# A diffusion-layer kernel on one core: the first modulation weights are loaded amid the tokens, their row is made between the sums of squares, and log, exp and the first products go segment by segment

## The chip, the cores and the metric

The kernel runs on one core of a Trainium2 chip. The metric is the device time of one execution in microseconds (us). Engines are named as in the profile: PE (matrix products), PEld (its weight loads), DVE (vector), ACT (scalar), POOL (GpSimd) and SP (which only issues DMAs here). Each engine works through its own instructions in the order in which they stand and waits for others by semaphores.

## What is computed

One layer over 1024 latent tokens and 256 context tokens of width 1024. The beginning, which the change touches, is this part of the reference:

```
mod_x = (jax.nn.silu(c) @ w_ada[i] + b_ada[i])[:, None, :]
mod_c = jax.nn.silu(c_ctx) @ w_ada[i] + b_ada[i]
sh1, sc1, g1, sh2, sc2, g2 = jnp.split(mod_x, 6, axis=-1)
csh1, csc1, cg1, csh2, csc2, cg2 = jnp.split(mod_c, 6, axis=-1)

px = modulate(rms_norm(x, norm1_w[i]), sh1, sc1) @ w_in[i]
pc = modulate(rms_norm(ctx, norm1_w[i]), csh1, csc1) @ w_in[i]
```

`rms_norm(x, w)` is `x * rsqrt(mean(x*x) + EPS) * w`, and `modulate(h, shift, scale)` is `h * (1 + scale) + shift`. Behind it come a gated DeltaNet on half of the heads, neighbourhood attention on the other half, an output projection and a SwiGLU network, none of which the change touches.

## The kernel before, in words

The tokens stand transposed: 8 tiles `xt0` to `xt7`, each with 128 of the 1024 channels as partitions and all 1280 tokens as columns (256 context tokens, then 1024 latent ones). The columns are worked on in three segments (`SEGS`) of 256, 512 and 512, since a bank of PSUM holds 512.

SP loads, in this order: the 8 token tiles (640 KB each, L680), the first two weight blocks `fraw0` and `fraw1` (512 KB each, L684), three tiles `wada` of modulation weights (1024 KB each, L676), two tables of constants, the other five `wada`, and small tables.

In the stage around the change, the order on PE, DVE and ACT is that of the code (a manual schedule); behind it a scheduler orders them.

- Sums of squares (L737 to L742). Token tiles go in pairs. ACT squares both, DVE adds the two squares, PE multiplies the sum with a matrix of ones, three matmuls (one per segment) that accumulate over the four pairs in three banks. In the last pair the second square and the addition go segment by segment.
- `rs` (L744, L745). ACT takes the logarithm of each segment's mean, and one exponential over all 1280 columns gives the reciprocal root.
- Weight split (L201, L204). A weight block is split into `whi` (rounded to the fast type) and `wlo` (the rest), on DVE for the first block, on POOL for the second.
- The row of tile j: `ada(j)` (L706) multiplies the two SiLU vectors with `wada` j on PE, and a copy (L708) takes the row `arow` out of PSUM. `column(j)` turns the row into columns with small PE matmuls (L714); DVE adds the bias (L716) and makes the scale `w1s` (L719).
- `normed_tile(k)`. DVE multiplies a token tile by `w1s` and `rs` (L726), ACT adds the shift and rounds to `hh` (L727), DVE makes the rest `hl` (L729). For tile 0 it goes over the three segments, for the others over 256 and 1024 columns.
- First products (L757). Two blocks of outputs, `first[0]` and `first[1]`, need for every tile k the products `whi`·`hh`, `wlo`·`hh` and `whi`·`hl`. For tile 0 they are written out in the stage itself, six matmuls for each of the three kinds, one block after the other. `ada(1)` stands ahead of them, `column(1)` and `normed_tile(1)` behind the first kind, `ada(2)` and `column(2)` behind the last.
- Then tiles 1 to 7 (L413), with `ada` 3 to 7 and their columns between the blocks (table `AHEAD`).

Of the kernel before, what the change touches and what calls it, by code (L numbers as in the profile page):

```python
# [9 lines left out]
F32 = mybir.dt.float32  # L10
# [3 lines left out]
AF = mybir.ActivationFunctionType  # L14
OP = mybir.AluOpType
# [73 lines left out]
def hybrid(ctx, tc, a, dbg):  # L89
# [293 lines left out]
    with ExitStack() as bs:  # L383
# [282 lines left out]
        with ExitStack() as xs:  # L666
            xp = pools(xs, "xp", "left")
            xt = []
# [5 lines left out]
            def load_ada(j):  # L674
                aw[j] = w = wap.tile([128, KT, 256], F32, name="wada", tag="wada")
                sp.dma_start(w, a["wa1"][j])  # L676

            for k in range(KT):
                x = xp.tile([128, T], F32, name=f"xt{k}", tag=f"xt{k}")
                sp.dma_start(x, a["xcT"][k])  # L680
                xt.append(x)
            raws = [xp.tile([128, KT, 128], F32, name=f"fraw{i}", tag=f"fraw{i}") for i in range(2)]
            for i in range(2):
                sp.dma_start(raws[i], a["w_conv"][4 + i])  # L684
            for j in range(3):
                load_ada(j)
# [33 lines left out]

            def normed_tile(k, cuts=(slice(0, CT), slice(CT, T))):
                t = xt[k]
                parts = [(x, mod1[:, k, int(x.start < CT):int(x.start < CT) + 1]) for x in cuts]
                for x, sh in parts:
                    j = int(x.start < CT)
                    dve.scalar_tensor_tensor(t[:, x], t[:, x], w1s[:, k, j:j + 1], rs[:, x], op0=OP.mult, op1=OP.mult)  # L726
                    act.activation(hh[k][:, x], t[:, x], AF.Identity, bias=sh)  # L727
                for x, sh in parts:
                    dve.scalar_tensor_tensor(hl[k][:, x], t[:, x], sh, hh[k][:, x].bitcast(F32),  # L729
                                             op0=OP.add, op1=OP.subtract)  # L730

            with tc.manual_schedule(engines={mybir.EngineType.PE, mybir.EngineType.DVE, mybir.EngineType.Activation}):
                sums = [bank() for _ in SEGS]
                segs = [slice(s0, s0 + n) for s0, n in SEGS]
                for k in range(0, KT, 2):
                    sq = [xp.tile([128, T], F32, name="sq%d" % i, tag="sq%d" % i, bufs=2 + i) for i in range(2)]
                    act.activation(sq[0], xt[k], AF.Square)  # L737
                    for s in segs if k == KT - 2 else [slice(0, T)]:
                        act.activation(sq[1][:, s], xt[k + 1][:, s], AF.Square)
                        dve.tensor_tensor(sq[1][:, s], sq[0][:, s], sq[1][:, s], OP.add)  # L740
                    for p, s in zip(sums, segs):
                        pe.matmul(p[:, :s.stop - s.start], M[C_ONE], sq[1][:, s], start=k == 0, stop=k == KT - 2)  # L742
                for p, s in zip(sums, segs):
                    act.activation(rs[:, s], p[:, :s.stop - s.start], AF.Ln, bias=b_eps, scale=1.0 / D)  # L744
                act.activation(rs, rs, AF.Exp, scale=-0.5)  # L745
                first[0].prefetch(raws[0], dve, dve)
                first[1].prefetch(raws[1], pool, pool)
                ada(0, dve.tensor_copy)
                column(0)
                normed_tile(0, segs)  # L750
                ada(1, act.copy)
                for b in first:
                    b.banks()
                for j, (w, x) in enumerate(((0, hh), (1, hh), (0, hl))):
                    for b in first:
                        for o, s in b.outs:
                            pe.matmul(o, b.w[w][:, 0], x[0][:, s], start=j == 0, stop=False)  # L757
                        if j == 0 and b is first[1]:
                            column(1)
                            normed_tile(1)  # L760
                ada(2, act.copy)
# [1062 lines left out]
```

## Time and profile before

| what | value |
|---|---|
| time, median of 3 runs | 1515.09 us (1510.95 to 1518.55) |
| the profiled execution's own time | 1512.36 us |
| its span in the trace | 1510.6 us |
| granted TensorE clock, mean | 0.996 |
| PE busy | 1462.2 us (97% of the span) |
| DVE, ACT, POOL busy | 996.8, 703.5, 236.7 us |
| instructions | 23890 |

The profile takes one execution. Its own time stands 1.76 us over its span. A row of its time line gives the start, the time from the first start to the last end of the group, the engine, the line of code, the operation, what it writes and reads, how many instructions were merged (`x3`), and in brackets how long the engine was idle just before and what ended that wait. A row of a table of stretches gives the stretch, its length, then for PE, PEld, DVE, ACT and POOL the busy time with the number of instructions, then the granted TensorE clock as a share of full speed, the share of the DMA engines that was busy, and GB/s.

### The profile page before, as it was taken

The numbers are of one execution on the slowest core, as the hardware profiler recorded it, in microseconds if no ns is written. First come the engines' busy times: TensorE is split into PE (matmuls) and PEld (weight loads), VectorE is DVE, ScalarE is ACT, GpSimd is POOL, SyncE is SP. The second block draws the span as 40 slices with busy tenths as digits, with TensorE's granted clock in tenths as the row PEclk, the third lists the DMA queues.
The fourth block names the chain that finished last, engine by engine and source line by source line (L and its number), as shares of the span: only waits on it lengthen the run. The fifth ranks groups of instructions, "written<-read, shape, count | busy, mean of one in ns | idle before, by whom it ended". The sixth has DMA issues, their size and how long they took to land.

```text
span 1510.6 us, 23890 instructions
## 1 busy us (share of the span) xinstructions
PE 1462.2 (97%) x8702; PEld 1223.5 (81%) x8702; DVE 996.8 (66%) x1716; ACT 703.5 (47%) x1389; POOL 236.7 (16%) x286
## 2 busy tenths in 40 slices
PE   6999999999999998999999999999999999999998
PEld 3788797877788877887878888888888888888887
DVE  5773589875463745778867389766665567598652
ACT  5453442456663246656853284333333334354440
POOL 1054601456652201111210000000000000000000
PEclk9999999999999999999999999999999999999999
DMA  9274122778665569998539205433333335798742
GB/s 389 75 215 143 54 78 72 244 222 248 195 191 174 157 187 291 290 263 279 163 112 343 79 28 166 141 105 105 105 105 105 105 105 174 260 360 279 251 140 84
DMA packets 205398, 267.36 MB, mean 177 GB/s; under 512 B 15968, under 2 KB 113760, under 8 KB 204256
## 3 DMA queue, kind: packets, MB, share of 16 engines
q1 hardware_dynamic: 197680, 260.01, 53.2%
q10 hardware_dynamic: 7600, 5.81, 1.2%
q8 instruction: 69, 1.13, 0.3%
q14 instruction: 49, 0.40, 0.1%
HBM read 201.02 MB, written 68.94 MB: 179 GB/s over the span
## 4 chain that ended last, share of the span: by engine, by line
PE 51%; ACT 1%; DVE 1%; issue 0%; DMA 0%; POOL 0%; DVEq 0%; POOLq 0%; ACTq 0%
PE ps L1398 28%; PE ps L1741 14%; PE ps L1527 3%; PE ps L1375 1%; PE ps L1549 1%; PE sc L332 1%; PE sc L322 1%; PE sc L309 1%; PE ps L1252 0%; PE ps L1261 0%; DMA z<-z_d 0%; ACT sq L1302 0%; ACT bt L315 0%; DVE bt L313 0%; PE ps L223 0%
## 5 line engine op out<-in xcount | busy, mean ns | idle before, releaser
L1459 ACT CAST uhi<-wq 128x512 fp32r<-128x512 f32 x101 | 61.3, 622 | 135.9 <-issue 84.6
L413 PE MATMUL blk<-hh,whi 128*128 128x512 f32 (+1 forms) x410 | 121.0, 389 | 1.6 <-ACT kk L562 1.4
L1459 ACT CAST uhi<-ws 128x512 fp32r<-128x512 f32 x91 | 54.0, 621 | 146.3 <-PE ps L1398 91.4
L413 PE MATMUL blk<-hl,whi 128*128 128x512 f32 (+1 forms) x410 | 113.4, 370 | 0.3 <-DVE hl L729 0.3
L609 PE MATMUL blk<-zw,hh 128*128 128x256 f32 (+1 forms) x576 | 112.3, 289 | 1.0 <-ACT cr L461 1.0
L413 PE MATMUL blk<-hh,wlo 128*128 128x512 f32 (+1 forms) x410 | 112.0, 370 | 0.6 <-POOL wlo L204 0.6
L1460 DVE TENSOR_TENSOR ulo<-wq,uhi 128x512 fp32r<-128x512 f32 x101 | 67.6, 688 | 59.1 <-ACT uhi L1459 32.7
L1398 PE MATMUL ps<-hT,uhi 128*128 128x512 f32 x336 | 103.7, 390 | 0.0
L1398 PE MATMUL ps<-lT,uhi 128*128 128x512 f32 x336 | 103.4, 389 | 0.0
L1398 PE MATMUL ps<-hT,ulo 128*128 128x512 f32 x336 | 103.4, 389 | 0.0
L609 PEld LDWEIGHTS blk<-zw,hh 128*128 128x128 f32 x576 | 90.7, 189 | 4.1 <-ACT cr L461 1.4
L1398 PE MATMUL ps<-hB,uhi 128*128 128x512 f32 x288 | 89.1, 390 | 0.0
L1398 PE MATMUL ps<-lB,uhi 128*128 128x512 f32 x288 | 88.7, 389 | 0.0
L1398 PE MATMUL ps<-hB,ulo 128*128 128x512 f32 x288 | 88.7, 389 | 0.0
L413 PEld LDWEIGHTS blk<-hh,wlo 128*128 128x128 f32 x410 | 71.0, 188 | 14.8 <-POOL wlo L204 0.9
L413 PEld LDWEIGHTS blk<-hl,whi 128*128 128x128 f32 x410 | 71.2, 188 | 14.4 <-DVE hl L729 0.8
L609 PE MATMUL blk<-zw,hl 128*128 128x256 f32 (+1 forms) x288 | 81.9, 284 | 0.0
L413 PEld LDWEIGHTS blk<-hh,whi 128*128 128x128 f32 x410 | 67.6, 190 | 16.8 <-issue 3.8
L204 POOL TENSOR_TENSOR wlo<-wraw,whi 128x1024 fp32r<-128x1024 f32 x18 | 44.8, 2488 | 186.8 <-ACT whi L203 186.5
L1398 PEld LDWEIGHTS ps<-lT,uhi 128*128 128x128 f32 x336 | 63.1, 188 | 13.1
L1398 PEld LDWEIGHTS ps<-hT,ulo 128*128 128x128 f32 x336 | 63.1, 188 | 13.1
L1398 PEld LDWEIGHTS ps<-hT,uhi 128*128 128x128 f32 x336 | 62.9, 188 | 13.0
(361 smaller groups left out, 3500.7 us busy)
## 6 DMA issues: line engine op xcount, KB each, us to landing
wq<-w_fo SPq DMA_DIRECT2D x99, 256.0 KB, 4.2
wq<-w_gu SPq DMA_DIRECT2D x88, 256.0 KB, 2.9
wad<-wa SPq DMA_DIRECT2D x64, 256.0 KB, 4.3
bt<-rpb SPq DMA_DIRECT2D x64, 192.0 KB, 3.9
t_d<-g SPq DMA_DIRECT2D x22, 512.0 KB, 3.5
fr<-t_d SPq DMA_DIRECT2D x44, 256.0 KB, 4.9
f_d<-g SPq DMA_DIRECT2D x33, 256.0 KB, 2.1
fr<-f_d SPq DMA_DIRECT2D x33, 256.0 KB, 4.2
```

The source lines that it names most:

```text
L204: lo_engine.tensor_tensor(o, r, h.bitcast(F32), OP.subtract)
L309: s = pe.matmul(sc[:, u * 640 + n0:u * 640 + n1], q, ks[i], start=i == 0, stop=i == 1)
L322: pe.transpose(sc[:, u * 640 + j * 128:u * 640 + (j + 1) * 128], bt[:, j * 128:(j + 1) * 128], ident)
L332: pe.matmul(sc[u * ND:u * ND + ND, 1280:1408], vv, pt[:, j * 128:(j + 1) * 128], start=j == 0, stop=j == 4)
L413: pe.matmul(o, ww[:, k], xx[k][:, s], start=k == 0 and j == 0, stop=k == KT - 1 and j == 2)
L609: pe.matmul(p[:, :c1 - c0], x[k][:, s], ww[:, k, c0:c1], start=k == 0 and j == 0, stop=k == KT - 1 and j == 2)
L1375: pe.matmul(o, w[wi][:, k], parts[xi][k][:, s], start=k == 4 and j == 0, stop=k == 3 and j == 2)
L1398: pe.matmul(o, w[wi][:, k], x[xi][:, k], start=first and k == 0 and j == 0, stop=k == n - 1 and j == 2, skip_group_check=True)
L1459: act.copy(hi, self.raw[key])
L1460: dve.tensor_tensor(lo, self.raw[key], hi.bitcast(F32), OP.subtract)
L1527: pe.matmul(o, w[wi][:, k], parts[xi][k][:, s], start=k == 0 and j == 0, stop=k == KT - 1 and j == 2)
L1741: pe.matmul(o[b], w[wi][:, b], F[xn, p][xi], start=n in (0, 1, 5) and p == 0 and j == 0, stop=p == NFB // 2 - 1 and j == 2, skip_group_che ...
```

## The change

Four things are done, all in the first stage; none of them adds or removes data that is loaded or a matmul.

1. SP issues the load of `wada` 0 behind the fourth token tile instead of behind the two weight blocks.
2. `ada(0)` and `column(0)` stand ahead of the third pair of token tiles instead of behind the exponential.
3. The exponential goes by segments, right behind the logarithm of its segment; and `high(0, segment)` (the L726 and L727 of before) is written between them.
4. The first products go segment by segment, both blocks in each; `ada(1)` moves behind the first kind of products, `column(1)` and `normed_tile(1)` behind the second kind.

```
             for k in range(KT):
+                if k == 4:
+                    load_ada(0)
                 x = xp.tile([128, T], F32, name=f"xt{k}", tag=f"xt{k}")
                 sp.dma_start(x, a["xcT"][k])
...
-            for j in range(3):
+            for j in range(1, 3):
                 load_ada(j)
...
+            def high(k, x):
+                t, j = xt[k], int(x.start < CT)
+                dve.scalar_tensor_tensor(t[:, x], t[:, x], w1s[:, k, j:j + 1], rs[:, x], op0=OP.mult, op1=OP.mult)
+                act.activation(hh[k][:, x], t[:, x], AF.Identity, bias=mod1[:, k, j:j + 1])
+
+            def low(k, x):
+                j = int(x.start < CT)
+                dve.scalar_tensor_tensor(hl[k][:, x], xt[k][:, x], mod1[:, k, j:j + 1], hh[k][:, x].bitcast(F32),
+                                         op0=OP.add, op1=OP.subtract)
...
                 for k in range(0, KT, 2):
+                    if k == 4:
+                        ada(0, dve.tensor_copy)
+                        column(0)
...
-                for p, s in zip(sums, segs):
-                    act.activation(rs[:, s], p[:, :s.stop - s.start], AF.Ln, bias=b_eps, scale=1.0 / D)
-                act.activation(rs, rs, AF.Exp, scale=-0.5)
                 first[0].prefetch(raws[0], dve, dve)
                 first[1].prefetch(raws[1], pool, pool)
-                ada(0, dve.tensor_copy)
-                column(0)
-                normed_tile(0, segs)
-                ada(1, act.copy)
+                for i, (p, s) in enumerate(zip(sums, segs)):
+                    act.activation(rs[:, s], p[:, :s.stop - s.start], AF.Ln, bias=b_eps, scale=1.0 / D)
+                    act.activation(rs[:, s], rs[:, s], AF.Exp, scale=-0.5)
+                    if i:
+                        high(0, segs[i - 1])
+                high(0, segs[2])
+                for s in segs:
+                    low(0, s)
                 for b in first:
                     b.banks()
                 for j, (w, x) in enumerate(((0, hh), (1, hh), (0, hl))):
-                    for b in first:
-                        for o, s in b.outs:
+                    for i in range(len(segs)):
+                        for b in first:
+                            o, s = b.outs[i]
                             pe.matmul(o, b.w[w][:, 0], x[0][:, s], start=j == 0, stop=False)
-                        if j == 0 and b is first[1]:
-                            column(1)
-                            normed_tile(1)
+                    if j == 0:
+                        ada(1, act.copy)
+                    if j == 1:
+                        column(1)
+                        normed_tile(1)
```

The first place is the third pair of token tiles, on DVE. `sq` are squares, `arow` and `pm` the row and its bank, `mod` the columns. Before:

```order
L740 TENSOR_TENSOR sq_196<-sq_195,sq_196 128x1280
L740 TENSOR_TENSOR sq_204<-sq_203,sq_204 128x1280
L740 TENSOR_TENSOR sq_212<-sq_211,sq_212 128x1280
L740 TENSOR_TENSOR sq_220<-sq_219,sq_220 128x256
L740 TENSOR_TENSOR sq_220<-sq_219,sq_220 128x512 x2
L201 CAST whi<-fraw_160 128x1024
L204 TENSOR_TENSOR wlo<-fraw_160,whi 128x1024
L708 COPY arow<-pm 128x256
L716 TENSOR_TENSOR mod_99<-pm,prm 128x2x2
L719 TENSOR_SCALAR w1s<-mod_99,prm 128x2
```

The same place on DVE in the changed kernel:

```order
L749 TENSOR_TENSOR sq_196<-sq_195,sq_196 128x1280
L749 TENSOR_TENSOR sq_204<-sq_203,sq_204 128x1280
L710 COPY arow<-pm 128x256
L718 TENSOR_TENSOR mod_99<-pm,prm 128x2x2
L721 TENSOR_SCALAR w1s<-mod_99,prm 128x2
L749 TENSOR_TENSOR sq_228<-sq_227,sq_228 128x1280
L749 TENSOR_TENSOR sq_236<-sq_235,sq_236 128x256
L749 TENSOR_TENSOR sq_236<-sq_235,sq_236 128x512 x2
L201 CAST whi<-fraw_162 128x1024
L204 TENSOR_TENSOR wlo<-fraw_162,whi 128x1024
```

The copy of row 0 and the two instructions on its columns moved ahead of the third and fourth additions of squares.

The second place is ACT between the last squares and the first `arow` copy of its own. `m` are the banks of the sums. Before:

```order
L744 ACTIVATE rs<-m,bias 128x256
L744 ACTIVATE rs<-m,bias 128x512 x2
L745 ACTIVATE rs<-rs 128x1280
L727 ACTIVATE hh_129<-xt_144,mod_99 128x256
L727 ACTIVATE hh_129<-xt_144,mod_99 128x512 x2
L708 COPY arow<-pm 128x256
```

The same place on ACT in the changed kernel:

```order
L755 ACTIVATE rs<-m,bias 128x256
L756 ACTIVATE rs<-rs 128x256
L755 ACTIVATE rs<-m,bias 128x512
L756 ACTIVATE rs<-rs 128x512
L726 ACTIVATE hh_129<-xt_144,mod_99 128x256
L755 ACTIVATE rs<-m,bias 128x512
L756 ACTIVATE rs<-rs 128x512
L726 ACTIVATE hh_129<-xt_144,mod_99 128x512 x2
L710 COPY arow<-pm 128x256
```

One exponential became three, and the first `hh` stands ahead of the last logarithm.

The third place is PE from the last sums to the first matmul of tile 1 (`hh_131`). Before:

```order
L706 MATMUL pm<-wada,wide 32x256 x8
L757 MATMUL blk<-hh_129,whi 128x256
L757 MATMUL blk<-hh_129,whi 128x512 x2
L757 MATMUL blk<-hh_129,whi 128x256
L757 MATMUL blk<-hh_129,whi 128x512 x2
L714 MATMUL pm<-bias,arow 128x2 x2
L757 MATMUL blk<-hh_129,wlo 128x256
L757 MATMUL blk<-hh_129,wlo 128x512 x2
```

The same place on PE in the changed kernel:

```order
L751 MATMUL m<-sq_236,ones 128x256
L751 MATMUL m<-sq_236,ones 128x512 x2
L768 MATMUL blk<-hh_129,whi 128x256 x2
L768 MATMUL blk<-hh_129,whi 128x512 x4
L708 MATMUL pm<-wada,wide 32x256 x8
L768 MATMUL blk<-hh_129,wlo 128x256 x2
L768 MATMUL blk<-hh_129,wlo 128x512 x4
L716 MATMUL pm<-bias,arow 128x2 x2
L768 MATMUL blk<-hl_130,whi 128x256 x2
```

Row 1 (`wada`) stands behind the six `whi`·`hh` products instead of ahead of them, and its columns (`bias`, `arow`) behind the `wlo` products. From tile 1 on, every engine has the same instructions in the same order as before.

14 lines of the change are left out of this document (4 added, 10 removed).

## The prediction

> **What bounds the kernel now.** I read the page first. PE is busy 97% of the span, and the chain of waits runs through PE. So a change counts by what it does to the time at which PE gets through its work. Next I read a table of stretches, to see where PE has room: behind each length stand PE's busy time and its instructions.
>
> ```profile
> 21.05:34.30 13.25, 11.27 (x76) 7.11 (x75) 8.53 (x16) 6.14 (x9) 2.75 (x1) 0.74 1.02 418
> 34.30:66.00 31.70, 31.36 (x223) 24.49 (x224) 22.05 (x37) 13.00 (x22) 0.00 (x0) 1.00 0.31 109
> ```
>
> From 34.3 to 66 PE idles 0.34 us. So the first 34 us decide: **the question is when tile 1's first product starts** (34.73 below). Behind it nothing moved on any engine, so the end shifts by the same amount unless a later wait absorbs it. Third, the time line of that stretch, engine by engine. Tokens on ACT:
>
> ```profile
> 11.96 1.27 ACT L737 ACTIVATE sq<-xt 128x1280 f32<-128x1280 f32 x1 [0.35 <-DMA xt<-xcT]
> 13.48 1.27 ACT L739 ACTIVATE sq<-xt 128x1280 f32<-128x1280 f32 x1 [0.25 <-DMA xt<-xcT]
> 15.14 1.27 ACT L737 ACTIVATE sq<-xt 128x1280 f32<-128x1280 f32 x1 [0.38 <-DMA xt<-xcT]
> 16.74 1.46 ACT L739 ACTIVATE sq<-xt 128x256 f32<-128x256 f32 x3 [0.33 <-DMA xt<-xcT]
> ```
>
> Every square waits for its tile: transfers set the pace here, one tile in 1.59 us ((16.74 - 11.96) / 3). Then the sums and the row on DVE and PE, with the weight loads at the start of the second, third and fourth sum:
>
> ```profile
> 14.02 0.19 PEld L742 LDWEIGHTS m<-sq,ones 128*128 128x128 f32 x1 [0.37 <-issue]
> ...
> 16.33 0.89 PEld L742 LDWEIGHTS m<-sq,ones 128*128 128x128 f32 x4 [0.40 <-DVE sq L740]
> ...
> 18.32 0.19 PEld L742 LDWEIGHTS m<-sq,ones 128*128 128x128 f32 x1 [0.24 <-issue]
> ...
> 14.79 1.49 DVE L740 TENSOR_TENSOR sq<-sq,sq 128x1280 f32<-128x1280 f32 x1 [1.65 <-ACT sq L739]
> 17.18 1.82 DVE L740 TENSOR_TENSOR sq<-sq,sq 128x256 f32<-128x256 f32 x3 [0.91 <-ACT sq L739]
> ...
> 21.81 1.07 PE L706 MATMUL pm<-wada,wide 128*32 128x256 f32 x16 [0.76 <-DMA wada<-wa]
> 22.94 0.42 DVE L708 COPY arow<-pm 128x256 f32<-128x256 f32 x1 [1.36 <-PE pm L706]
> 23.42 0.61 PE L714 MATMUL pm<-bias,arow 128*128 128x2 f32 x4 [0.54 <-DVE arow L708]
> 24.26 0.23 DVE L719 TENSOR_SCALAR w1s<-mod,prm 128x2 f32<-128x2 f32 x1
> ```
>
> One sum takes PE about 2.15 us; row 0 takes 2.68 us from its first matmul to `w1s` (21.81 to 24.49). Then the logarithms, the exponential, and the products:
>
> ```profile
> 19.38 0.47 ACT L744 ACTIVATE rs<-m,bias 128x256 f32<-128x256 f32 x1 [1.19 <-PE m L742]
> ...
> 21.09 0.69 ACT L744 ACTIVATE rs<-m,bias 128x512 f32<-128x512 f32 x1 [0.17 <-PE m L742]
> 21.81 1.27 ACT L745 ACTIVATE rs<-rs 128x1280 f32<-128x1280 f32 x1
> 25.11 0.51 ACT L727 ACTIVATE hh<-xt,mod 128x256 fp32r<-128x256 f32 x1 [2.03 <-DVE xt L726]
> 25.77 1.38 ACT L727 ACTIVATE hh<-xt,mod 128x512 fp32r<-128x512 f32 x2 [0.15 <-DVE xt L726]
> ...
> 24.22 1.94 PE L706 MATMUL pm<-wada,wide 128*32 128x256 f32 x16 [0.19 <-DMA wada<-wa]
> 26.09 2.98 PE L757 MATMUL blk<-hh,whi 128*128 128x256 f32 x6
> 28.87 0.85 PE L714 MATMUL pm<-bias,arow 128*128 128x2 f32 x4
> 29.58 2.02 PE L757 MATMUL blk<-hh,wlo 128*128 128x256 f32 x6
> ...
> 32.70 1.07 PE L706 MATMUL pm<-wada,wide 128*32 128x256 f32 x16
> ...
> 34.73 0.83 PE L413 MATMUL blk<-hh,whi 128*128 128x256 f32 x3
> ```
>
> The last `hh` ends at 27.15; `column(1)` follows at 28.87. The same sixteen matmuls of a row take 1.94 us at 24.22 and 1.07 at 32.70: the clock. It is the second last number of a table row, and these rows show what goes before half clock:
>
> ```profile
> 95.78:99.19 3.41, 1.74 (x9) 1.12 (x9) 3.41 (x7) 1.70 (x3) 3.10 (x8) 1.00 0.70 221
> 20.69:24.10 3.41, 2.04 (x21) 1.02 (x20) 1.35 (x3) 2.19 (x3) 3.11 (x1) 1.00 1.00 416
> 24.10:27.51 3.41, 3.29 (x19) 1.47 (x20) 3.28 (x8) 2.15 (x4) 0.00 (x0) 0.50 1.03 417
> 27.51:30.92 3.41, 3.41 (x12) 2.93 (x12) 1.71 (x5) 0.18 (x1) 0.00 (x0) 0.50 1.01 419
> 290.34:293.75 3.41, 1.40 (x10) 0.98 (x9) 2.46 (x4) 3.21 (x5) 2.50 (x3) 1.00 0.99 319
> ```
>
> Half clock lasts from 24.10 to 30.92, twice 3.41 us, behind a stretch with 2.04 us of PE work, most of it small matmuls. It comes again behind 290.34 (1.40 us). Behind 95.78 (1.74 us, nine matmuls) it doesn't. So I take the clock to be set every 3.41 us by the work in the stretch before: half when a stretch holds under about 1.5 us of full matmuls, whole again after a full one.
>
> **The change, step by step.** *Load.* `wada` 0 has 1024 KB, a token tile 640 KB, so it takes 1.59 x 1024 / 640 = 2.55 us and lands near 12.9. Tiles 4 to 7 land that much later: their squares start at 14.5, 16.0, 17.7 and 19.3. `fraw` slips by 2.55 us too (the weight block on POOL becomes ready near 26.4 instead of 23.8, long before the `wlo` products). `wada` 1 and all behind it keep their times, for the bytes ahead of them are the same. Bounds for the delay are nothing and 2.55 us; I take 2.55, since the squares wait for DMA at each step. By the next step either end gives nearly the same.
>
> *Row 0 amid the sums.* PE ends the second sum near 16.2 (14.02 + 2.15). Then row 0 takes its 2.68 us: `w1s` is done at 18.9. This adds a wait: on DVE the copy of the row waits for PE, and behind it stand the third and fourth additions of squares, for which PE waits. The third addition could start at 17.3 (16.0 + 1.27) but starts at **18.8 instead of 14.79**; it ends at 20.3, the fourth at 22.1. At full clock the third sum starts on PE at 20.3 and the fourth at 22.4 (before: 18.32), **+4.1 us**.
>
> *Clock, first time.* In the stretch from 17.28 to 20.69 PE has only the columns (0.6 us of tiny matmuls) and 0.4 us of the third sum. So half clock from 20.69 to 24.10, which the sums fill. Of 4.3 us of work 0.4 is done before and 1.7 within; the fourth sum starts at 24.2, **1.8 us more**.
>
> *Log and exp.* The first logarithm starts 1.06 us behind the fourth sum (19.38 - 18.32): 25.3. Exponentials of 256 and 512 aren't in the trace. The nearest rows bound them: the logarithms (0.47, 0.69) and `hh` (0.51, 0.72 in rows 25.11 and 25.77 for two); I take the latter, and the ends are 0.1 us apart. They sum to 1.95 us against 1.27. In the new order ACT ends the first `hh` at 28.3 (25.3 + 0.47 + 0.51 + 0.69 + 0.72 + 0.51), the second at 30.3, and the last, behind one more DVE step of 0.75, at **31.2 instead of 27.15**. Taking row 0 and half an exponential off this path gains about 2 us of the 5.9 lost above.
>
> *Products of tile 0.* By segments they start at 28.3, 30.3 and 31.2. In the stretch 27.51 to 30.92 PE then has two pairs, under 1 us: less than the 1.40 that went before half clock at 293.75. So **half clock again** from 30.92. The last pair ends at 32.2. `ada(1)`, which filled a wait before, now follows: 1.94 us, 34.1. The `wlo` products at half clock take 2.4 (36.5). `column(1)` ends near 37.3 (before: 29.72), and DVE starts tile 1 only then. From there the chain is as before (29.75 to 34.73, 4.98 us): scale, `hh`, and behind it on ACT the copy of row 2, which PE's `column(2)` awaits. Since `ada(2)` is done earlier beside it, I count 4.6: tile 1 starts at **41.8 instead of 34.73, +7.1 us**.
>
> *Edits at nothing.* The split of `fraw0` (2.63 us on DVE) stands beside the sums on PE, 22.1 to 24.7; at full clock throughout, it would hold the first `hh` by 0.7. The pairing of blocks reorders six matmuls.
>
> *Behind it.* Waits of PE for DMA hardly exist: the longest list entry is below. So at most 1.9 us can be absorbed, and that load follows a store of the same chain; I count none.
>
> ```profile
> PE ps L1261 <- DMA y<-y_d: 1.9, 1, 1.9
> ```
>
> **Rivals.**
>
> (A) *One slow stretch.* The two early pairs of products suffice to keep the clock, as 1.74 us did at 95.78. Then the steps from 31.2 run at full clock: last pair 31.7, `ada(1)` 32.7, `wlo` 33.9, and tile 1 at 38.8: +4.1 us, 1516.5. For it: I have no row between 1.40 and 1.74, nor one with so few matmuls. Against: the two pairs are under 1 us.
>
> (B) *No slow stretch.* Without both, tile 1 starts at 37.1: +2.4 us, 1514.8. Against: at 24.10 the clock fell though PE's longest wait before was 0.76 us. The Trainium skill gives a rule that ends here, in TensorE: Matmul & The Clock Gate, section "HAM oscillation — how this bites in real kernels": "no PE-idle gaps >~3.4µs". By that rule none of the new gaps (about 2 us each) would slow the clock. The row at 20.69 contradicts it, and the measurement decides.
>
> (C) *Another grid.* The stretches of 3.41 us need not lie alike to the program in each execution. Shifted by a third, the slow stretch covers all of the sums, and a second one the products: up to +10.5, 1522.9. The Trainium skill says in TensorE: Matmul & The Clock Gate, section "Part 1: The HAM clock gate (the "warmup" mystery)", that the window is 3413 ns and free-running; the trace agrees in the length, twice 3.41, and one trace can't show the rest.
>
> (D) *Not slower.* The place is the third addition of squares on DVE. If it started near 14.8 as before, because load and row cost the sums nothing, the gain side would be left: `hh` ends at 25.2 (logarithm and exponential by segments from 19.38), `column(1)` ends at 28.5, tile 1 starts at 33.8: -0.9 us, 1511.5. The change gains only if that addition starts before 15.7. Against: `w1s` can't be done before 18.6 with the second sum ending at 16.2, and DVE takes its instructions in order.
>
> **How the numbers follow.** Own time of the profiled execution 1512.36 + 7.1 = 1519.5. The median shown is 2.7 above that execution, which makes 1522.2 on its base; I predict the middle, 1521. Chances: forecast (+5.5 to +9) 0.48, A 0.25, B 0.10, C 0.12, D 0.05. The range goes from B on the lower base, less 1.8 for a part of D, 1513, to C on the higher base, 1526. A measurement of this kernel can tell about 0.5%, 7.6 us, from no change. The forecast lies just under that bound: I put 0.24 of its 0.48 above it, with all of C, so 0.36 slower. No case is faster by that much; 0.02 for the spread of the runs (1510.95 to 1518.55) on top of D; 0.62 within.
>
> **What would show it.** Right: the third addition of squares starts at 18.5 to 19, behind `w1s`; clock 0.5 at 21 to 24 and again from about 31; first `hh` product near 28, `column(1)` near 36.5, tile 1 near 42. Wrong: tile 1 under 38 with full clock (B), or an addition near 15 (D); then my account of the clock or of the transfers fails. A wait behind 66 us that shrinks by several us would also prove the carry to the end wrong.

## The result, and the profile after

The changed kernel takes **1521.88 us** (median of 6 runs, 1519.51 to 1523.99). The kernel before, run beside it, takes 1515.76 us (6 runs, 1510.95 to 1518.55). The ratio is 1.0046, with a 95% interval of 1.003 to 1.0062: slower by about 6 us. The interval does not hold 1, so the loss is there, but it is far under the 2% from which a change is called slower here. The forecast was 1521. One execution of `m1_warm` (5131 us) and one of the kernel before beside it (8250 us) were several times slower than all others and are in no ratio below. The profiled execution's own time is 1523.99 us, its span 1522.2 us, its mean clock 0.993.

First the time line of PE in the changed kernel, from the first sums to tile 1:

```profile
10.51 6.77 PE L751 MATMUL m<-sq,ones 128*128 128x256 f32 x12 [10.51 <-DVE sq L749]
17.20 1.07 PE L708 MATMUL pm<-wada,wide 128*32 128x256 f32 x16
18.82 0.61 PE L716 MATMUL pm<-bias,arow 128*128 128x2 f32 x4 [0.55 <-DVE arow L710]
21.34 6.26 PE L751 MATMUL m<-sq,ones 128*128 128x256 f32 x12 [1.91 <-DVE sq L749]
28.67 0.50 PE L768 MATMUL blk<-hh,whi 128*128 128x256 f32 x2 [1.07 <-ACT hh L726]
30.52 0.73 PE L768 MATMUL blk<-hh,whi 128*128 128x512 f32 x2 [1.34 <-ACT hh L726]
31.44 0.73 PE L768 MATMUL blk<-hh,whi 128*128 128x512 f32 x2 [0.19 <-ACT hh L726]
32.11 1.94 PE L708 MATMUL pm<-wada,wide 128*32 128x256 f32 x16
33.97 2.10 PE L768 MATMUL blk<-hh,wlo 128*128 128x256 f32 x6
35.92 0.50 PE L716 MATMUL pm<-bias,arow 128*128 128x2 f32 x4
...
40.56 0.84 PE L413 MATMUL blk<-hh,whi 128*128 128x256 f32 x3
```

Tile 1 starts at 40.56, 5.83 us later than before (34.73), where the forecast said 7.1. The last two sums end at 27.60 (21.34 + 6.26), `column(1)` starts at 35.92. Then ACT:

```profile
14.71 1.27 ACT L746 ACTIVATE sq<-xt 128x1280 f32<-128x1280 f32 x1 [2.86 <-DMA xt<-xcT]
16.23 1.27 ACT L748 ACTIVATE sq<-xt 128x1280 f32<-128x1280 f32 x1 [0.26 <-DMA xt<-xcT]
...
25.92 0.47 ACT L755 ACTIVATE rs<-m,bias 128x256 f32<-128x256 f32 x1 [5.00 <-PE m L751]
26.43 0.42 ACT L756 ACTIVATE rs<-rs 128x256 f32<-128x256 f32 x1
...
28.11 0.51 ACT L726 ACTIVATE hh<-xt,mod 128x256 fp32r<-128x256 f32 x1
...
30.67 0.72 ACT L726 ACTIVATE hh<-xt,mod 128x512 fp32r<-128x512 f32 x1 [0.21 <-DVE xt L725]
```

The first square behind the new load waits 2.86 us for its tile, and the last `hh` ends at 31.39. DVE, and POOL below it:

```profile
18.34 0.42 DVE L710 COPY arow<-pm 128x256 f32<-128x256 f32 x1 [4.97 <-PE pm L708]
...
19.80 3.86 DVE L749 TENSOR_TENSOR sq<-sq,sq 128x1280 f32<-128x1280 f32 x4
23.59 2.83 DVE L201 CAST whi<-fraw 128x1024 fp32r<-128x1024 f32 x1
26.45 1.23 DVE L204 TENSOR_TENSOR wlo<-fraw,whi 128x1024 fp32r<-128x1024 f32 x1
27.59 1.32 DVE L725 SCALAR_TENSOR_TENSOR xt<-xt,w1s,rs 128x256 f32<-128x256 f32 x2
```

```profile
21.99 1.13 POOL L201 CAST whi<-fraw 128x1024 fp32r<-128x1024 f32 x1 [16.46 <-DMA fraw<-w_conv]
23.20 2.67 POOL L204 TENSOR_TENSOR wlo<-fraw,whi 128x1024 fp32r<-128x1024 f32 x1
```

The third addition of squares starts at 19.80. What nobody had asked about stands in the third row: the cast of the first weight block takes 2.83 us where it took 0.69 before (18.92). It lies beside POOL's split of the second block, which ran at 19.24 before, behind the additions. Of the four additions the last, beside POOL's cast, takes 1.53 us instead of 0.69. Last, the stretches of 3.41 us, cut where the clock changes (columns as above):

```profile
18.41:21.82 3.41, 1.09 (x6) 0.98 (x7) 2.67 (x6) 2.19 (x4) 0.00 (x0) 1.00 1.04 422
21.82:25.23 3.41, 3.41 (x6) 1.38 (x5) 3.41 (x3) 0.00 (x0) 3.16 (x2) 0.50 1.00 414
25.23:28.64 3.41, 2.37 (x7) 0.95 (x5) 3.29 (x4) 2.65 (x6) 0.64 (x1) 1.00 1.05 427
28.64:32.05 3.41, 1.84 (x6) 0.89 (x6) 2.44 (x5) 2.51 (x4) 0.00 (x0) 1.00 1.02 423
32.05:35.46 3.41, 3.41 (x22) 1.89 (x22) 0.31 (x1) 0.37 (x1) 0.00 (x0) 0.50 1.00 416
```

Both slow stretches that the forecast named came, behind stretches with 1.09 and 1.84 us of PE work. The second lasted 3.41 us, not twice that. From tile 1 on PE is as full as before:

```profile
40.13:71.83 31.70, 31.39 (x222) 24.50 (x223) 22.83 (x37) 13.00 (x22) 0.00 (x0) 1.00 0.13 37
```

31.39 us busy of 31.70, against 31.36 before. So the first stage costs 5.83 us. The profiled executions differ by more (1522.2 - 1510.6 = 11.6); the other 5.8 are taken up under "What the runs showed".

### The profile page after: what moved, and what is told of

Read it like the earlier page. It is cut to its first block, busy times and chain, and to the rows that moved or that the text cites. A ratio compares the mean times of both kernels' runs of the same rounds, so it can differ in the third digit from the quotient of the medians.

```text
span 1522.2 us, 23892 instructions
## 1 busy us (share of the span) xinstructions
PE 1467.7 (96%) x8702; PEld 1226.2 (81%) x8702; DVE 998.5 (66%) x1716; ACT 703.4 (46%) x1391; POOL 236.2 (16%) x286
## 4 chain that ended last, share of the span: by engine, by line
PE 51%; ACT 1%; DVE 0%; issue 0%; DVEq 0%; ACTq 0%
PE ps L1411 28%; PE ps L1754 14%; PE ps L1540 3%; PE ps L1388 1%; PE ps L1562 1%; PE sc L332 1%; PE sc L309 1%; PE sc L322 1%; PE ps L1286 0%; PE ps L1265 0%; PE ps L1274 0%; ACT sq L1315 0%; DVE bt L313 0%; PE ps L223 0%; ACT pt L325 0%; PE ps L1291 0%
```

## The experiments

The **placement theory** is that of the forecast: most of the loss is where the load and the two rows now stand, and the clock adds to it. The **clock theory**, its rival: the loss comes from TensorE's half clock, and with the whole clock the new order would cost little. After the first runs a third was put beside them, the **POOL theory**: POOL's split, now beside the additions, holds DVE. The measure that separates them is the start of tile 1, since from there all kernels do the same work. It is read from one traced execution of each kernel and has an error of its own. `p3`, `p4` and `c2` below have the same code as the kernel before up to the last sum, and yet that sum ends at 21.75, 22.30 and 22.64 us, against 21.05 before, because in those executions the sums begin later or their first matmuls stay slow for longer. So a difference at tile 1 counts only as far as it arises behind that point, or is larger than 1.6 us. The four `p` runs have one time each, beside 1514.43 us for one run of the kernel before. The ratios of the others are to 30 or 34 runs of it.

### The parts alone, put into the kernel before

`p1_load` has the early load and nothing else:

```diff
             for k in range(KT):
+                if k == 4:
+                    load_ada(0)
...
-            for j in range(3):
+            for j in range(1, 3):
```

> The kernel before with the first of the four parts alone: the load of wada 0 stands behind the fourth token tile. Placement theory (each part loses by itself, since what it moves stands in front of something that is awaited): token tiles 4 to 7 land 2.6 us later, the last sum ends 2.6 us later (23.5 instead of 21.0), row 0 then follows without its wait for the transfer (0.76 us), and tile 1 starts near 36.0, between 35.0 and 37.5 by where half clock falls, against 34.73 before. Clock theory (the loss of the whole change is half clock, and moved pieces cost nothing while the clock is whole): tile 1 at 34 to 35 unless a stretch of half clock more than before is seen.

Measured: 1515.89 us; tile 1 at 37.94, 3.2 us behind the kernel before. The third addition of squares starts at 17.29, 2.50 us later (14.79 before), as the tiles do, and row 0 runs behind the sums at 23.33 rather than at 21.81. The transfer's delay of one load is on the path. The last sum ends 2.35 us later. Tile 1 is later than the expected 35.0 to 37.5 by 0.4; the likely reason is that half clock (29.0 to 35.8) lies on the products to their end here.

`p2_load_row` has, besides, row 0 between the sums:

```diff
                 for k in range(0, KT, 2):
+                    if k == 4:
+                        ada(0, dve.tensor_copy)
+                        column(0)
...
-                ada(0, dve.tensor_copy)
-                column(0)
```

> The kernel before with the first two parts: load of wada 0 behind the fourth token tile, and row 0 with its columns ahead of the third pair. Placement theory: the third addition of squares starts behind w1s near 19 to 20, a stretch of half clock falls on the sums, the last sum ends near 26.8, tile 1 starts near 39.0 (37.7 to 40.2). Clock theory: as far as the sums run at whole clock, tile 1 starts at 36 or earlier; the difference to p1_load is the half clock stretch alone.

Measured: 1520.7 us; tile 1 at 41.77, later than in the whole change, and missed by 2.8 us. The third addition starts at 20.45, 3.16 us behind that of `p1_load`. Its four additions then take 6.01 us in one row; before, they take 3.31 (1.49 + 1.82). That row led to the POOL theory. There are also 10.2 us of half clock before tile 1, against 6.8 before, so the 2.8 aren't POOL's alone.

`p3_seg` has the logarithm, the exponential and `high` by segments:

```diff
-                for p, s in zip(sums, segs):
-                    act.activation(rs[:, s], p[:, :s.stop - s.start], AF.Ln, bias=b_eps, scale=1.0 / D)
-                act.activation(rs, rs, AF.Exp, scale=-0.5)
...
-                normed_tile(0, segs)
+                for i, (p, s) in enumerate(zip(sums, segs)):
+                    act.activation(rs[:, s], p[:, :s.stop - s.start], AF.Ln, bias=b_eps, scale=1.0 / D)
+                    act.activation(rs[:, s], rs[:, s], AF.Exp, scale=-0.5)
+                    if i:
+                        high(0, segs[i - 1])
+                high(0, segs[2])
```

> The kernel before with the third part alone: logarithm and exponential by segments, the first hh ahead of the last logarithm, row 0 ahead of them as before. Placement theory: three exponentials cost ACT 0.5 to 0.7 us more than one and the hh between them holds the last logarithm, so the last hh ends 1.3 us later (28.4 instead of 27.15), and tile 1 starts near 35.9 (35.1 to 36.8). Rival (segments help, since the first segment is ready earlier): the first hh ends before 25.6 and tile 1 starts at or before 34.7.

Measured: 1520.56 us; tile 1 at 37.39, 0.6 us behind the expected window. The last `hh` ends at 28.79 (27.15 before), and 0.70 of these 1.64 us were there at the end of the last sum already (21.75). With row 0 behind the sums, the first `hh` waits for `w1s`, and behind it on ACT wait the last logarithm and exponential, which were done early before.

`p4_prod` has the products by segments and row 1 moved:

```diff
-                ada(1, act.copy)
...
-                    for b in first:
-                        for o, s in b.outs:
+                    for i in range(len(segs)):
+                        for b in first:
+                            o, s = b.outs[i]
...
-                        if j == 0 and b is first[1]:
-                            column(1)
-                            normed_tile(1)
+                    if j == 0:
+                        ada(1, act.copy)
+                    if j == 1:
+                        column(1)
+                        normed_tile(1)
```

> The kernel before with the fourth part alone: first products by segments, row 1 behind the first kind, its columns and normed tile 1 behind the second kind. Placement theory: products start 0.5 us earlier, but column 1 comes near 32 instead of 28.9, and tile 1 starts near 36.4 (35.4 to 38.4). Clock theory: tile 1 starts at 34.5 to 35 unless a stretch of half clock more is seen.

Measured: 1521.65 us; tile 1 at 37.67, `column(1)` at 33.03 (28.87 before). In its execution the last sum ends at 22.30, 1.25 us later than before, though nothing ahead of it was changed, so the 2.9 at tile 1 is too much for the edit: 1.7 of it arises behind the sums.

All of `p1`, `p3` and `p4` have 6.8 us of half clock before tile 1, as the kernel before has, and still start tile 1 by 2.7 to 3.2 us later (`p3` and `p4` by 2.0 and 1.7 without their later sums). That speaks for the placement theory. These prices don't add up to the whole (5.83). Each edit also shifts the same work into another stretch of the clock; how much that makes wasn't measured.

### Parts taken back out of the change

`u1_row1_back` puts row 1 back, ahead of the products; `u2_row0_late` puts row 0 back, behind the sums; `u3_rows_back` does both:

```diff
                     low(0, s)
+                ada(1, act.copy)
...
                     if j == 0:
-                        ada(1, act.copy)
-                    if j == 1:
                         column(1)
```

```diff
                 for k in range(0, KT, 2):
-                    if k == 4:
-                        ada(0, dve.tensor_copy)
-                        column(0)
...
                 first[1].prefetch(raws[1], pool, pool)
+                ada(0, dve.tensor_copy)
+                column(0)
```

> The changed kernel with row 1 put back: ada 1 ahead of the first products, its columns and normed tile 1 right behind the first kind of products; the rest of the change stays. Placement theory: tile 1 starts near 38.8 (37.7 to 39.5) instead of 40.56, for the columns of row 1 come some 3 us earlier. Rival (what tile 1 waits for is the last hh alone, and row 1 is beside the path): tile 1 within 0.5 us of 40.56.

Measured: 1518.68 us, ratio 1.0024 [1.0011, 1.0038]; tile 1 at 39.89, outside both expectations. The second sum on PE ended at 18.69 here, 1.41 us later than in the changed kernel (17.28), so row 0 and the additions behind it came later by 1.41, and so did the last sum (29.01). From there to tile 1 it takes 10.88 us instead of 12.96: row 1 put back gains 2.1 us, of which 0.67 is left at tile 1.

> The changed kernel with row 0 and its columns put back behind the sums, ahead of the logarithms; its load stays amid the tokens, the segments stay. Placement theory: the third addition of squares starts at 17.3 instead of 19.8 and the last sum ends near 23.5 instead of 27, but row 0 then stands between sums and hh; tile 1 near 39.7 (38.2 to 41.5), so 1 us better than the change with a wide spread by the clock. Rival (the addition held by row 0 is the main loss): tile 1 at 37 to 38.

Measured: 1519.82 us, ratio 1.0026 [1.0011, 1.0041]; tile 1 at 39.27. The third addition starts at 17.38, near that of `p1_load`, and the last sum ends at 23.49 instead of 27.60; row 0 and the logarithms behind it take most of that back.

> The changed kernel with both modulation rows where the kernel before has them; the early load, the log and exp by segments and the first products by segments remain. If the price of each row's new place is what u1_row1_back and u2_row0_late showed (0.7 and 1.3 us at tile 1's beginning), tile 1 begins at 38.6 (37.7 to 39.3), 3.9 us behind the kernel before, and the median is 1518.5. If the rows carry the whole price between them, it begins at 35.0 to 36.0 and the median is within 1 us of the kernel before.

Measured: 1517.66 us, ratio 1.0014 [0.9999, 1.0028]; tile 1 at 37.34, between the two expected windows. Taken back together the rows are worth 3.2 us of the 5.83 at tile 1, with 3.4 us of half clock before it instead of 6.8. What is left, 2.61, is about the early load's 2.50.

### The clock taken out

`c2_before_fill` and `c1_after_fill` put short matmuls on constants into PE's waits, whose results nobody reads:

```diff
+            def fill(n):
+                p = bank("pm")
+                for _ in range(n):
+                    pe.matmul(p[:, :128], ones, ones, start=True, stop=True)
...
+                fill(3)
                 ada(0, dve.tensor_copy)
+                fill(2)
                 column(0)
+                fill(3)
```

> The kernel before with the same small matmuls: 3 ahead of row 0, 2 behind it, 3 behind its columns. Clock theory: no half clock from 20 to 34 us, tile 1 starts at 32.7 to 33.5 instead of 34.73. If so, the difference between this and c1_after_fill (about 4.5 us) is what the order of the waits costs without the clock. Rival: half clock stays since the small matmuls count too little; tile 1 at 34.7 to 35.5.

Measured: 1515.43 us, ratio 0.9996 [0.9981, 1.001]; no half clock between 16.7 and tile 1, but tile 1 at 34.48. PE shows why:

```profile
10.89 11.75 PE L747 MATMUL m<-sq,ones 128*128 128x256 f32 x24 [10.89 <-DVE sq L745]
22.48 0.83 PE L735 MATMUL pm<-ones 128*128 128x128 f32 x6
23.24 1.07 PE L706 MATMUL pm<-wada,wide 128*32 128x256 f32 x16
```

The sums, which stand ahead of all fillers, end at 22.64 (10.89 + 11.75) instead of 21.05: they began slowly, as under "What the runs showed". The fillers add 0.6 us, where before row 0 waited 0.76 us for its load. From the end of the last sum to tile 1 it takes 11.84 us instead of 13.68. So without half clock this part is 1.84 us shorter, and the start of this execution hid it.

In the changed kernel they stand around row 0 (2 and 9), ahead of the products (8) and between their segments (6 and 2):

> The changed kernel with small matmuls of ones with ones into a bank that nothing reads (0.2 us each at whole clock), put where PE only waits: 2 behind row 0, 9 behind its columns, 8 ahead of the first products, 6 and 2 between their segments. Clock theory (two stretches of half clock, brought about by little PE work, cost the changed kernel 3 to 5 us by themselves): no half clock from 17 to 40 us, the sums take 4.3 us instead of 5.8, tile 1 starts at 37 to 38 instead of 40.56, 3 us off. Placement theory (the order of the waits alone costs it): the fillers don't matter or delay by up to 1 us, tile 1 at 40.5 to 41.5.

Measured: 1521.1 us, ratio 1.0039 [1.0024, 1.0053]; tile 1 at 39.92, between the two expectations. There is no half clock between the first sums and tile 1. At tile 1 only 0.64 us are gained. But the first sums began more slowly here too: row 0 starts at 18.10 instead of 17.20, and the third addition at 20.70 instead of 19.80. From that addition to tile 1 it takes 19.22 us instead of 20.76, so the clock is worth 1.54 us of it. The kernel before loses about as much by its half clock (1.84 in `c2`), so the clock doesn't make the difference of the two kernels: the clock theory falls. DVE's time line and its grouped rows show what else is on the path:

```profile
20.70 6.01 DVE L756 TENSOR_TENSOR sq<-sq,sq 128x1280 f32<-128x1280 f32 x4
...
L756 DVE TENSOR_TENSOR sq<-sq,sq 128x256 f32<-128x256 f32 x1 | 1.3, 1259 | 0.0
L756 DVE TENSOR_TENSOR sq<-sq,sq 128x512 f32<-128x512 f32 x1 | 2.8, 2828 | 0.0
```

An addition of 512 columns takes 2.83 us in place of 0.69. POOL's rows of the same execution:

```profile
21.59 1.48 POOL L201 CAST whi<-fraw 128x1024 fp32r<-128x1024 f32 x1 [15.72 <-DMA fraw<-w_conv]
23.16 2.40 POOL L204 TENSOR_TENSOR wlo<-fraw,whi 128x1024 fp32r<-128x1024 f32 x1
```

The two long additions lie beside these two. `c3_fill_no_pool` is `c1_after_fill` with POOL's split taken away (the high half is cast on ACT at 21.74, the low half subtracted on DVE, later):

```diff
-                first[1].prefetch(raws[1], pool, pool)
+                later = Later()
+                first[1].prefetch(raws[1], later)
...
                 high(0, segs[2])
+                dve.tensor_tensor(*later.args)
```

> The changed kernel with the filler matmuls of c1_after_fill, and in addition the split of the second weight block is taken off POOL: its high half is cast on ACT behind the last squares, its low half subtracted on DVE behind the high halves. POOL theory: DVE's additions of squares take 0.42 and 0.69 us again (6.0 us for the four in c1 become about 3.3), the last sum ends about 2.7 us earlier, near 25.4, the first log begins near 26, and tile 1 begins at 37.5 (36.8 to 38.5) instead of c1's 39.92. Rival, the additions are slow for another reason (the bigger program, the fillers): they stay at 5.5 us or more and tile 1 stays at 39.5 or later.

Measured: 1518.76 us, ratio 1.0031 [1.0017, 1.0044]; tile 1 at 37.63. DVE and PE:

```profile
19.93 3.02 DVE L760 TENSOR_TENSOR sq<-sq,sq 128x1280 f32<-128x1280 f32 x4
...
L760 DVE TENSOR_TENSOR sq<-sq,sq 128x512 f32<-128x512 f32 x2 | 1.3, 682 | 0.0
```

```profile
21.52 4.52 PE L762 MATMUL m<-sq,ones 128*128 128x256 f32 x12
...
32.99 0.50 PE L716 MATMUL pm<-bias,arow 128*128 128x2 f32 x4
...
37.63 0.83 PE L413 MATMUL blk<-hh,whi 128*128 128x256 f32 x3
```

The additions are short again (682 ns), the last sum ends at 26.04 instead of 28.14, and tile 1 starts 2.29 us earlier. Of these, 0.77 were there at the third addition already (19.93 instead of 20.70), by the start of the execution. From it to tile 1 it takes 17.70 us instead of 19.22. The POOL theory holds, and its price on this path is about 1.5 us with the whole clock. The median can't show it: 1.0031 against 1.0039 lies within the intervals.

`m1_warm` gives the kernel before the same whole clock, with fillers that also run ahead of the first sums:

```diff
+                fill(26)
                 sums = [bank() for _ in SEGS]
...
+                fill(3)
                 ada(0, dve.tensor_copy)
+                fill(2)
                 column(0)
+                fill(2)
```

> The kernel before with 26 filler matmuls ahead of the first sums of squares, so that TensorE is busy before its first real work, and some 8 around row 0. Clock theory: the clock is whole by the time of the sums in every execution, the sums end near 20.8, no half clock falls between 20 and 33, and tile 1 begins at 33.0 (32.3 to 33.8) instead of 34.73; the median is 2 us below the kernel before (ratio 0.9987). Rival, the fillers delay what they stand ahead of (as in c2_before_fill): tile 1 begins at 34.5 or later and the ratio is 1.000.

Measured: 1514.56 us, ratio 0.9999 [0.9985, 1.0013]; tile 1 at 32.89, as expected. PE:

```profile
10.90 4.74 PE L748 MATMUL m<-sq,ones 128*128 128x256 f32 x12 [1.48 <-DVE sq L746]
16.19 4.56 PE L748 MATMUL m<-sq,ones 128*128 128x256 f32 x12 [0.55 <-DVE sq L746]
...
27.98 0.51 PE L714 MATMUL pm<-bias,arow 128*128 128x2 f32 x4
...
32.89 0.84 PE L413 MATMUL blk<-hh,whi 128*128 128x256 f32 x3
```

The last sum ends at 20.75, only 0.3 us earlier than before, though the second ends 1.1 us earlier: here the third waits for DVE. The gain of 1.84 us at tile 1 can't be told in the median: the interval holds both it and nothing.

`m2_warm_seg` adds the products by segments, row 1 left where it was:

```diff
-                    for b in first:
-                        for o, s in b.outs:
+                    for i in range(len(segs)):
+                        for b in first:
+                            o, s = b.outs[i]
...
-                        if j == 0 and b is first[1]:
-                            column(1)
-                            normed_tile(1)
+                    if j == 0:
+                        column(1)
+                        normed_tile(1)
```

> m1_warm with the first products of tile 0 segment by segment, row 1 staying behind them as in the kernel before. Products theory: without the rows' move the segment order starts the products earlier but ends with the last segment all the same, so tile 1 begins within 0.4 us of m1_warm, and the median within 0.5 us of it. Rival, the order of the products costs by itself: tile 1 begins 1 us or more behind m1_warm.

Measured: 1513.36 us, ratio 0.9992 [0.9979, 1.0006]; tile 1 at 32.44, 0.45 us ahead of `m1_warm`. So the segment order of the products is not what costs; by itself it gains a little, though the total isn't told from no change.

### The sum, at the whole clock

`m1_warm` (the order of before) and `c3_fill_no_pool` (the order of after) both run without half clock before tile 1 and without POOL in the way of the additions. Their difference is the price of the order, with one reservation given below the table (times in us):

| start or end | before | after | m1_warm | c3_fill_no_pool | c3 less m1 |
|---|---|---|---|---|---|
| second sum ends on PE | 16.76 | 17.28 | 15.64 | 17.41 | +1.77 |
| third addition of squares starts | 14.79 | 19.80 | 14.64 | 19.93 | +5.29 |
| last sum ends on PE | 21.05 | 27.60 | 20.75 | 26.04 | +5.29 |
| last `hh` of tile 0 ends | 27.15 | 31.39 | 27.01 | 29.75 | +2.74 |
| `column(1)` starts | 28.87 | 35.92 | 27.98 | 32.99 | +5.01 |
| tile 1 starts | 34.73 | 40.56 | 32.89 | 37.63 | **+4.74** |
| third addition to tile 1 | 19.94 | 20.76 | 18.25 | 17.70 | -0.55 |

The load and row 0 delay the sums by 5.29. Row 0 off the path and the exponential by segments give 2.55 back. `column(1)`, behind row 1 and the `wlo` products, loses 2.27 again. The rest of the 5.83 is the difference of the disturbances: clock and POOL cost the changed kernel 2.93 us (40.56 - 37.63), the clock costs the kernel before 1.84 (34.73 - 32.89). Two things blur the pair. `c3` waits about 0.3 us for fillers ahead of its last products. And `m1` warms PE ahead of the first sums, `c3` doesn't: its second sum ends 1.77 us later. In the order of after this counts in full, since the third addition stands behind row 0 and row 0 behind that sum: it starts 2.5 us behind the sum's end in all five kernels with row 0 amid the sums (17.28 and 19.80 in the changed kernel, 18.69 and 21.21 in `u1_row1_back`, 17.41 and 19.93 here). In the order of before it waits for the tokens and not for PE. So with a warm start as well, the price of the order would be about 3.0 us, as an estimate (4.74 - 1.77). `c2` and `c1`, whose second sums end alike (18.34 and 18.17), give 39.92 - 34.48 = 5.44, and about 3.9 without POOL's 1.5. All three say that the order costs more than half of the 5.83; which of them is nearest depends on how the start falls.

## Why the prediction was right, step by step

*Load*: right. The squares start at 14.71 and 16.23, forecast 14.5 and 16.0; alone it moves the third addition by 2.50 us, forecast 2.55.

*Row 0 amid the sums*: the mechanism was right, the size 1.0 us short: 19.80, forecast 18.8. The term at fault is "PE ends the second sum near 16.2". It ended at 17.28. Half of that miss is a misread row: 14.02 is where the second sum's weights were loaded, and PE was still at the first sum then, so that the second ended at 16.76 even before. The other half is that the first matmuls stayed slow for longer. Grouped rows of 13 to 15 us, before and after, the last two numbers of the first part being busy us and mean ns:

```profile
L742 PE MATMUL m<-sq,ones 128*128 128x512 f32 x4 | 2.7, 779 | 0.0
```

```profile
L751 PE MATMUL m<-sq,ones 128*128 128x512 f32 x3 | 2.8, 1056 | 0.0
```

At full clock one takes 592 ns. This start is the same code in both kernels; the clock became whole at 13.86 us in the one execution and at 14.98 in the other.

*Clock, first time*: right. The half clock came behind the stretch with 1.09 us of work, at 21.82 in place of 20.69. Its price of 1.8 can't be read off alone, since DVE was held at the same time; counted from the third addition, `c1_after_fill` and `c3_fill_no_pool` put 1.54 us to the half clock of the whole stage and 1.5 more to POOL.

*Log and exp*: right to 0.2 us (last `hh` at 31.39, forecast 31.2), partly by luck. The first logarithm was 0.6 late, and DVE's split ended at 27.68 and held the first scale by 0.7 us (the exponential ends at 26.85).

*Edits at nothing*: **this step failed.** The forecast asked when POOL's block would be ready (near 26.4; it was 25.87) and not what POOL does to the engine beside it. Row 0 moved the additions and the cast into POOL's 3.9 us, where the cast took 2.83 us instead of 0.69; at the whole clock the hold costs about 1.5 us (`c3_fill_no_pool`). The forecast also named the 0.7 us that the split on DVE could cost, but for the case of a whole clock; it came with half clock and for another reason.

*Products of tile 0*: the order of events was right, the rule behind its clock was not. By "under about 1.5 us" the stretch with 1.84 us of work should have kept the clock, and it fell; the forecast had counted under 1 us, for stretches that lie 1.1 us earlier. That half clock came here all the same is luck, and how much work keeps the clock stays open. The rest: products, `ada(1)` at 1.94 us, `wlo`, `column(1)` at 35.92 (forecast near 36.5). Too large was the clock's term: one stretch of half clock (32.05 to 35.46) in place of two, so `column(1)` ended at 36.42, not 37.3. From there to tile 1 it took 4.1 us, not 4.6, so tile 1 came at 40.56, not 41.8.

*Behind it*: right for the program; the 5.83 are still there at 73.47 (67.64 before). The waits of PE for DMA have no new entry to speak of:

```profile
PE ps L1274 <- DMA y<-y_d: 2.2, 1, 2.2
```

So the misses, the 1.0 of row 0 and the hold on DVE on one side, one stretch of the clock and the shorter last part on the other, cancelled to 1.2 us at tile 1. The total was nearer still, partly by luck: 1521 was the middle between sums on two bases (1519.5 and 1522.2), and the 5.83 of tile 1 on the median now beside it (1515.76) makes 1521.6.

*Rivals.* (A) and (B) would have put tile 1 at 38.8 and 37.1; with 1.84 us of PE work in a stretch the clock still fell. The rule quoted there from the Trainium skill, TensorE: Matmul & The Clock Gate, "HAM oscillation — how this bites in real kernels", is contradicted again: the longest wait of PE ahead of 21.82 is 1.91 us. (C) is seen in the other runs: half clock behind the first sums and before tile 1 makes 6.8 us in the changed kernel and between 3.4 and 10.2 in the runs without fillers. (D) needed the third addition before 15.7; it came at 19.80.

## What to carry to other kernels

A row that is moved "into a gap" stands in three in-order queues, and everything behind it in each queue moves too; price the queue where the next wait of the path ends (here DVE's additions), not the gap. Before moving work on one engine, look at which engine runs beside its new place: here a cast of 0.69 us took 2.83 beside POOL's subtraction, which had been off the path. And compare two orders at the same clock, with fillers in both, before giving a cause to the clock; look first whether both executions began alike, and count from the last event that the edit can't have moved.

## What the runs showed of the hardware that was not expected

**POOL holds DVE.** Beside POOL's cast and subtraction, DVE's additions of 256 and 512 columns took 1.26 and 2.83 us instead of 0.42 and 0.69, and the cast of 1024 columns 2.83 instead of 0.69. A held operation ends a fixed time behind POOL's: in the changed kernel POOL's subtraction ends at 25.87 and DVE's cast at 26.42, 0.55 us later, and the held additions of 512 columns end 0.55 behind POOL's in `c1`, `p2` and `u1` too, those of 256 columns 0.28. That is 0.14 us less than they take alone, so nearly all of their work came behind POOL's end. The kernel before has it as well, off the path: DVE's subtraction took 1.94 us there, and 1.23 where POOL was done. The Trainium skill, SBUF — State Buffer, section "SBUF: two separate sides", calls the port pair that DVE and GpSimd share "an exclusive lock, not a bandwidth split"; among DVE's operations it names those with two SBUF inputs and those in a two-port mode, and whichever engine starts first has the pair for its whole instruction. These rows agree with that, and `c3_fill_no_pool`, where POOL is idle, has 682 ns.

**The beginning is slow though the clock column says 1.00.** The first 512-column matmuls take 1061 ns, later ones 592. The trace's records of the granted clock begin where the matmuls turn fast, at 13.86 us in the kernel before and 14.98 in the changed one, a whole number of 3.41 us ahead of the later changes; the column counts the time ahead of the first record as 1.00. In the runs without fillers ahead the first record stands between 13.86 and 17.15 us. With fillers ahead (`m1_warm`) it stands at 5.89, and none of the sums' matmuls takes over 593 ns.

**Where the spread of the runs comes from.** Behind tile 1 every one of these kernels has the same work, but not the same half clock. Stretches of before, then of after:

```profile
264.00:272.00 8.00, 8.00 (x48) 6.73 (x47) 6.07 (x7) 6.14 (x9) 0.00 (x0) 1.00 0.34 82
290.00:300.00 10.00, 7.99 (x35) 6.35 (x33) 8.26 (x10) 7.73 (x13) 8.54 (x9) 0.83 1.01 322
572.00:580.00 8.00, 7.99 (x78) 7.33 (x77) 4.88 (x16) 6.51 (x23) 1.23 (x2) 1.00 0.84 265
```

```profile
264.00:272.00 8.00, 6.37 (x30) 4.94 (x29) 7.72 (x12) 3.63 (x7) 0.19 (x1) 0.79 0.55 150
300.00:308.00 8.00, 8.00 (x40) 6.80 (x41) 5.57 (x6) 6.34 (x14) 7.79 (x8) 0.79 1.03 334
572.00:580.00 8.00, 5.50 (x35) 4.47 (x32) 1.44 (x6) 2.91 (x8) 0.31 (x1) 0.79 0.87 310
596.00:606.00 10.00, 6.74 (x51) 5.81 (x51) 6.91 (x23) 4.97 (x10) 1.30 (x3) 0.83 0.72 197
```

The clock is a mean over each row, so 0.83 over 10 us and 0.79 over 8 us are one stretch of 3.4 us at half. The profiled execution of before has one such stretch behind tile 1, that of after four (one that begins in the last 2 us of a span is not counted here). The rest of the span, from tile 1 to the end, goes with them over the kernels' profiled executions:

| half clock behind tile 1 | rest of the span, us |
|---|---|
| 3.4 us (before) | 1475.9 |
| 6.8 us (p1, p2, u1, u2, m1, c3) | 1476.2, 1477.1, 1476.9, 1477.2, 1476.9, 1478.6 |
| 10.2 us (m2) | 1479.2 |
| 13.6 to 13.7 us (u3, c1, p3, after) | 1480.0, 1480.8, 1481.4, 1481.6 |
| 17.1 us (p4, c2) | 1482.2, 1481.5 |

From 3.4 to 17.1 the rest grows by about 6 us, some 0.45 us for each us of half clock. For the 10.2 us that the profiled execution of after has more, that makes 4.6 of the 5.8 us beyond the first stage; the other 1.2 is no more than rows with equal half clock differ by (1476.2 to 1478.6). All recorded runs say the same: each has its time and its mean clock, and a straight line through the 65 of the kernel before, which spread from 1509.9 to 1522.7 us, gives 0.42 us for each us of half clock. At an equal clock the 6 runs of the changed kernel lie 5.1 us above that line, about the first stage alone. Their mean clock is a little lower (0.9942 against 0.9955, some 4 us more of half clock). Whether the change brings that about, or chance in 6 runs, stays open, as does what sets the place of the grid in an execution.
